# Keys' groups: the squares of the values' weights behind the seventh high part and the first snapshot, their scale behind the seventh low part

## The chip, the cores and the metric

The kernel runs on one core of a Trainium2 chip. The metric is the device time of one execution in microseconds, as the median of several runs. TensorE is PE in the profile, VectorE is DVE, ScalarE is ACT, GpSimd is POOL, SyncE is SP.

## The reference

Two decoder layers over 512 tokens of width 2048. Each layer normalises its input, sends it through one input projection, and feeds three groups of heads: a gated short convolution, stick-breaking attention with 8 heads, and gated linear attention with 4 heads. The three outputs are joined, go through an output projection and are added to the input. Cut to what matters here:

```python
h = _rmsnorm(x, norm_g)
proj = h @ w_in                       # [512, 2048] x [2048, 7696]
(cv_h, cv_b, cv_c, cv_g,
 sb_q, sb_k, sb_v, sb_g,
 gl_q, gl_k, gl_v, gl_g, gl_lr) = jnp.split(proj, split_points, axis=-1)
...
q = _rmsnorm(sb_q.reshape(b, s, SB_HEADS, SB_HD), sb_qn_g)
k = _rmsnorm(sb_k.reshape(b, s, SB_HEADS, SB_HD), sb_kn_g)
v = sb_v.reshape(b, s, SB_HEADS, SB_HD)
y_sb = _stick_breaking(q, k, v) * jax.nn.silu(sb_g)
...
mix = jnp.concatenate([y_conv, y_sb, y_gla], axis=-1)
return x + mix @ w_out
```

All is in float32, and the kernel reaches that precision with float16 matmuls.

## The kernel before, in words

**Groups.** The weights are taken in groups of 256 columns, in an order fixed in `specs` and `names`. In each layer, for each of the four pairs of attention heads j, the groups come as `v j` (values), `g j` (gate), `q j` (queries), `k j` (keys). Behind `k 3` comes `conv h 1`. So behind each of the eight keys' groups (four in each of two layers) stands a group whose weights are not of the quick kind: `v 1`, `v 2`, `v 3` or `conv h 1`. The text calls them the values' weights.

**High and low parts.** A float32 weight is scaled by a power of two and split into a float16 high part (ACT, a scaled copy) and a float16 low part (DVE, the scaled weight minus the high part). The scale comes from the sum of the squares of the group's weights: two squares on ACT with accumulators (`wmax`, L383), a reduction over the partitions on POOL (`wscale`, L399), and four small operations on DVE (L402 to L417).

**Two kinds of groups.** A plain group has two high parts and two low parts of 128x2048 (L454, L461), and `project_toks` multiplies with them, 192 matmuls (L712 to L714, or L701 to L703 where columns come first). A quick group (queries, keys, gates) uses a Strassen-like scheme with seven products on half-size blocks. `wsums` forms sums of weight blocks in place on DVE (L516 to L532) and splits seven blocks into high and low parts of 128x1024 (L507, L508). The seventh has buffers of its own, `w7h` and `w7l`; its input comes from the sum on L532. `project_quick` makes the seven products (L796 for queries and keys, 48 matmuls each; L793 where columns come first) in two PSUM banks. Between them ACT takes snapshots of partial sums (L808, L812, L815) and DVE combines (L809, L816 to L821). The first snapshot reads what product 1 left, in a bank shared with product 2, and product 5 goes on accumulating there. The second reads what product 4 left, and product 7 goes on there.

**What runs beside a keys' group.** While TensorE works on `k j`, ACT and DVE finish the splits of the keys' own weights, square and scale the queries (L1361, L1379, L1383, L1384), and prepare the next group's weights: squares, scale, parts. Weights are staged in two buffers (`st`); the load of the group after next (L362, issued by POOL) waits until the seventh low part, the last reader of the buffer, is done. Behind the group the keys are squared (L1361), scaled, split (L1383, L1384) and transposed by DMA (L1388), and the scores of the heads (L1270) need them.

**What sets the order.** Nothing of this part is placed by hand. A planner runs the program through a timeline of its own and fills each engine's queue by priority; `tc.high_priority()` lifts the squares, the scale and the parts of the next group above the rest. `order(a, b)` only says that the planner must not place `a` ahead of `b`: it makes no semaphore. `weights()` leaves two hooks for the group, called by the projection as it emits its matmuls. The first hook emits the squares of the next group's weights (`squares`), the second their scale and parts (`parts_of`), each ordered behind the matmul that it is given. In `project_quick` the first hook is called at the third matmul of product 1, the second after product 2:

```python
if start and t == kk == 0 and i == 2 and o is pa:
    hook(mm)
...
prod(pa, w11, a11, True)
hook(prod(pb, wT2, s_, False))
S.activation(y12, za, AF.Copy)
```

Of the kernel before, what the change touches and what calls it, by code (L numbers as in the profile page):

```python
# [10 lines left out]
AF = mybir.ActivationFunctionType  # L11
ALU = mybir.AluOpType
# [31 lines left out]
def hybrid_trunk(ctx, tc, x, norm_g, w_in, conv_w, conv_b, sb_qn_g, sb_kn_g,  # L44
                 gla_w_up, gla_b_up, gla_on_g, w_out, out):
    nc = tc.nc
    V, S, G, T = nc.vector, nc.scalar, nc.gpsimd, nc.tensor
# [27 lines left out]
    def sm(n, tag, bufs=None):  # L75
        return small.tile([P, n], F32, tag=tag, name=nm(tag), bufs=bufs or 1 + (tag in TWICE))
# [7 lines left out]
    def bank(pool, tag):  # L84
        return pool.tile([P, 512], F32, tag=tag, name=nm("ps" + tag))
# [109 lines left out]
    def order(a, b):  # L195
        tc.add_manual_dep(a.ins, b.ins.name, mybir.DependencyInfo(
            mybir.DependencyClass.NoSync, mybir.DependencyReason.DATA), reason="order")
# [119 lines left out]
    names = []  # L317
# [25 lines left out]
    loaded = {}  # L343
    cursor = [0]

    staged, whole, narrow, peak, scales = {}, {}, {}, {}, {}

    def junk(n):

# [42 lines left out]
    def wscale(i):  # L392

        l, src, cols = specs[i]

        m = sm(1, "wq")
        if i:
            gm = sm(2 + (i in narrow), "wgm")
            G.partition_all_reduce(gm, peak.pop(i), P, RED.add)  # L399
            if i in narrow:  # L400
                V.tensor_tensor(gm[:, 0:1], gm[:, 0:1], gm[:, 2:3], ALU.add)
            first = V.tensor_tensor(m, gm[:, 0:1], gm[:, 1:2], ALU.add)  # L402
        else:

            ps = bank(psm, "m")[:, :1]
            pk = peak.pop(i)
            first = None
            for j, (a, b) in enumerate(((ones, pk[:, 0:1]), (ones, pk[:, 1:2]), (pk[:, 2:3], pk[:, 2:3]))):
                T.matmul(ps, a.to_broadcast([P, P]), b, start=j == 0, stop=j == 2)
            V.tensor_scalar(m, ps, 2.0 ** -120, None, ALU.max)  # L410
        V.tensor_scalar(m.bitcast(I32), m.bitcast(I32), 0x7F000000, 1, ALU.bitwise_and, ALU.logical_shift_right)

        lift = int(i in quick)
        sc = sm(1, "ws")
        V.tensor_scalar(sc.bitcast(I32), m.bitcast(I32), -1.0, float((204 - lift) << 23), ALU.mult, ALU.add)  # L415
        u = sm(1, "wu", bufs=6)
        V.tensor_scalar(u.bitcast(I32), m.bitcast(I32), (outoff[l] if src is w_out else inoff)[lift][:, l:l + 1],  # L417
                        None, ALU.add)
        loaded[i] = ([], u)
        scales[i] = sc  # L420
        return first
# [37 lines left out]
    def wlo(i, h):  # L459
        wh, wl = loaded[i][0][h]  # L460
        V.scalar_tensor_tensor(wl[:, :, :GW], staged[i][h], scales[i], wh[:, :, :GW], ALU.mult, ALU.subtract)  # L461
        if i in narrow:
            V.scalar_tensor_tensor(wl[:, :, GW:], narrow[i][:, h * HK:(h + 1) * HK, :], scales[i], wh[:, :, GW:],
                                   ALU.mult, ALU.subtract)

    def squares(i, mm):

        with tc.high_priority():
            for h in range(2):
                a = wmax(i, h)  # L470
                if not h:
                    order(a, mm)
                if ksq:
                    order(a, ksq[0])
            ksq.clear()

    def parts_of(i, mm):

        with tc.high_priority():
            order(wscale(i), mm)  # L480
            if i in quick:
                wsums(i)
                return
            for h in range(2):
                whi(i, h)
                wlo(i, h)

    def hook(mm):

        if hooks:  # L490
            hooks.pop(0)(mm)

    def wsums(i):

        sc = scales[i]
        b11, b12, b21, b22 = (whole[i][:, r::2, c * P:(c + 1) * P] for r in range(2) for c in range(2))
        parts = loaded[i][0]
        for _ in range(3):
            a = [wpool.tile([P, HK, GX], F16, tag=t, name=nm(t)).rearrange("p k c -> p (k c)") for t in ("wh", "wl")]
            parts.extend([p_[:, n * HK * P:(n + 1) * HK * P] for p_ in a] for n in range(2))  # L500
        parts.append([wk([P, HK * P], t, 1, dt=F16) for t in ("w7h", "w7l")])
        for n in range(7):
            parts[n] = [a.rearrange("p (k c) -> p k c", c=P) for a in parts[n]]

        def split(b, n):
            h_, l_ = parts[n]
            hi = S.activation(h_, b, AF.Copy, scale=sc)  # L507
            V.scalar_tensor_tensor(l_, b, sc, h_, ALU.mult, ALU.subtract)  # L508
            return hi


        if specs[i][1] is w_out:
            split(b11, 0)
            V.tensor_tensor(b11, b11, b12, ALU.add)
            split(b22, 2)
            V.tensor_tensor(b12, b12, b22, ALU.add)  # L516
            V.tensor_tensor(b22, b11, b22, ALU.add)
            split(b22, 1)
            split(b12, 3)
            V.tensor_tensor(b22, b22, b21, ALU.add)  # L520
            split(b21, 4)
            split(b11, 5)
            split(b22, 6)
            return
        split(b11, 0)
        split(b22, 2)
        V.tensor_tensor(b22, b12, b22, ALU.add)  # L527
        split(b22, 1)
        V.tensor_tensor(b11, b22, b11, ALU.subtract)
        split(b11, 3)  # L530
        split(b21, 4)
        V.tensor_tensor(b21, b22, b21, ALU.add)  # L532
        split(b12, 5)
        split(b21, 6)
# [150 lines left out]
    for l in range(depth):  # L685
# [92 lines left out]
        def project_quick(src, sums, y, cols):  # L778

            (w11, wT2, w22, wT3, w21, wt1, wT4), u = weights()  # L780
            (pa, pb), (pd, pf) = ([bk[:, n * GW:(n + 1) * GW] for n in range(2)]
                                  for bk in [bank(psp, "p") for _ in range(2)])
            a11, a12, a22 = ([a[:, 2 * r:2 * r + 2, c::2, :] for a in src] for r, c in ((0, 0), (0, 1), (1, 1)))
            s_, a21_22, a12_s, a11_21 = sums

            def prod(o, w, a, start, stop=False):
                for t in range(1 if cols else 2):
                    for kk in range(HK):
                        for i, (p_, q_) in enumerate(((0, 0), (0, 1), (1, 0))):
                            st_ = start and t == kk == i == 0  # L790
                            en = stop and kk == HK - 1 and i == 2
                            if cols:
                                mm = T.matmul(o, w[q_][:, kk, :], a[p_][:, :, kk, :], start=st_, stop=en,  # L793
                                              skip_group_check=True)
                            else:
                                mm = T.matmul(o[:, t * P:(t + 1) * P], a[p_][:, t, kk, :], w[q_][:, kk, :], start=st_,  # L796
                                              stop=en, skip_group_check=True)
                            if start and t == kk == 0 and i == 2 and o is pa:
                                hook(mm)
                return mm  # L800

            y11, y12, y21, y22 = (
                y[:, c, r * GW:(r + 1) * GW] if cols else y[:, 2 * r:2 * r + 2, c * P:(c + 1) * P]
                for r in range(2) for c in range(2))
            za, zb, zd, zf = (a if cols else a.rearrange("p (t c) -> p t c", c=P) for a in (pa, pb, pd, pf))
            prod(pa, w11, a11, True)
            hook(prod(pb, wT2, s_, False))
            S.activation(y12, za, AF.Copy)  # L808
            V.tensor_tensor(y21, zb, y12, ALU.subtract)  # L809
            prod(pf, w22, a12_s, True)  # L810
            prod(pd, wT3, a11_21, False)
            S.activation(y22, zd, AF.Copy)  # L812
            prod(pa, w21, a12, False)
            prod(pb, wt1, a21_22, False, True)
            S.activation(y11, za, AF.Copy)  # L815
            V.tensor_tensor(y12, zb, y12, ALU.subtract)  # L816
            V.tensor_tensor(y22, y12, y22, ALU.subtract)
            lastmm[0] = prod(pd, wT4, a22, False, True)
            V.tensor_tensor(y12, zf, y12, ALU.add)
            yield 0, u  # L820
            V.tensor_tensor(y21, zd, y21, ALU.subtract)  # L821
            yield 2, u
# [148 lines left out]
        for p in range(2):  # L971
# [3 lines left out]
            a = wk([P, seq], "ga")  # L975
# [26 lines left out]
        for tag in ("qT", "kT"):  # L1002
            o = wk([P, 2, seq], tag)
# [14 lines left out]
            s_ = sm(1, "gas")  # L1018
# [42 lines left out]
        for p in range(2):  # L1061
# [4 lines left out]
            for li, h in enumerate(LEV[:-1]):  # L1066
                b = li % 2
# [32 lines left out]
            hi, lo = src16[1]  # L1100
# [38 lines left out]
            for a, o in zip(ax, (aps[:, :, :256], aps[:, :, 256:], aps2[:, :, :256])):  # L1139
                hi, lo = (a[:, i].rearrange("p (h c) -> p h c", h=2) for i in range(2))  # L1140
# [179 lines left out]
        for j in range(4):  # L1320
# [17 lines left out]
            s_ = mixscale(2 + j, m, "b", 12.0)  # L1338
# [3 lines left out]
            for n in range(2):  # L1342
# [11 lines left out]
                for b in range(2):  # L1354
# [4 lines left out]
                    for i in range(4):  # L1359
                        cs = slice(i * P, (i + 1) * P)  # L1360
                        a = S.activation(e[:, cs], rb.rearrange("p a c -> p (a c)")[:, cs], AF.Square,  # L1361
                                         accum_out=sq[:, 8 * n + 4 * b + i:8 * n + 4 * b + i + 1])
# [117 lines left out]
```

## Time and profile before

| | |
|---|---|
| median of 3 runs | 1647.73 us (1642.52 to 1655.6) |
| profiled execution, own time | 1646.43 us |
| its span | 1644.6 us |
| busy share of the span | PE 98%, DVE 87%, ACT 72%, POOL 16% |
| granted TensorE clock | 1.000 |

Times inside the profile count from the start of the span. In a timeline each row has the start, the duration, the engine, the line, the operation with what it writes and reads, the shapes, the count, and in brackets the idle time ahead of it with what ended it. Matmuls overlap in the pipeline, so 48 of them take less than 48 times the duration of one.

### The profile page before, as it was taken

The page shows a single profiled execution, that of the slowest core. Times are in us where ns is not written, and L with a number is a line of the kernel's source. Part 1 is how long each engine was busy: PE and PEld are TensorE (multiplying, and loading weights), DVE is VectorE, ACT ScalarE, POOL GpSimd, SP SyncE. Part 2 cuts the span into 40 slices and gives each one's busy share as a digit, 9 for nine tenths or more (in the row PEclk, how much of TensorE's full clock was granted, in tenths as well). Part 3 has the DMA queues.
Part 4 walks back from the last instruction along what each step waited for, and adds up shares of the span by engine and source line. Part 5 has one row for each costly group of instructions (what it writes and reads, how often), then busy time and mean ns, then how long its engine had stood idle before and what let it go on. Part 6 is the DMA issues. An engine that isn't in the chain of part 4 may idle for free.

```text
span 1644.6 us, 41938 instructions
## 1 busy us (share of the span) xinstructions
PE 1619.6 (98%) x18058; PEld 1356.1 (82%) x18058; DVE 1433.7 (87%) x2403; ACT 1192.3 (72%) x1763; POOL 270.7 (16%) x300
## 2 busy tenths in 40 slices
PE   8999999999999999999999999999999999999999
PEld 5757768989899967799986668689898989768998
DVE  7989989989898979898699899898988889878893
ACT  7668887977777776756766788788777878666571
POOL 0122021211112121111102111211121212110110
PEclk9999999999999999999999999999999999999999
DMA  7154435477868677544643544546776776894441
GB/s 260 54 129 140 93 118 114 108 160 142 166 149 167 149 167 197 171 155 142 203 120 105 129 116 116 140 83 140 151 157 153 158 158 155 174 196 141 155 155 53
DMA packets 195995, 235.97 MB, mean 143 GB/s; under 512 B 90259, under 2 KB 156125, under 8 KB 195297
## 3 DMA queue, kind: packets, MB, share of 16 engines
q0 software_dynamic: 79072, 178.27, 41.2%
q1 hardware_dynamic: 107728, 45.56, 14.6%
q10 hardware_dynamic: 9008, 9.45, 1.8%
q8 instruction: 141, 2.31, 0.6%
q14 instruction: 46, 0.37, 0.1%
HBM read 179.65 MB, written 14.68 MB: 118 GB/s over the span
## 4 chain that ended last, share of the span: by engine, by line
PE 33%; DVE 10%; ACT 4%; DMA 3%; issue 2%; SPq 0%; POOL 0%; DVEq 0%; ACTq 0%; POOLq 0%
PE psp L796 11%; PE psp L793 6%; PE psp L843 4%; PE psp L714 2%; PE psp L713 2%; PE psp L712 2%; DVE wl L508 2%; PE psp L702 1%; PE psp L701 1%; PE psp L703 1%; DMA m<-mixd 1%; ACT wh L507 1%; ACT junk L383 1%; DMA kT<-raw 1%; DVE wl L461 1%
## 5 line engine op out<-in xcount | busy, mean ns | idle before, releaser
L507 ACT ACTIVATE wh<-st,ws 128x1024 f16<-128x1024 f32 x264 | 293.8, 1144 | 168.3 <-DVE st L527 89.8
L508 DVE SCALAR_TENSOR_TENSOR wl<-st,ws,wh 128x1024 f16<-128x1024 f32 x264 | 332.1, 1280 | 24.0 <-ACT wh L507 23.8
L383 ACT ACTIVATE junk<-st 128x2048 uint8<-128x2048 f32 x150 | 285.5, 1903 | 19.4 <-DMA st<-in_w_out_dram 10.4
L793 PE MATMUL psp<-s,wh 128*128 128x256 f16 x1280 | 217.7, 273 | 0.0
L793 PEld LDWEIGHTS <-wh 128*128 128x128 f16 x1920 | 187.4, 98 | 23.4 <-issue 1.4
L796 PE MATMUL psp<-wh,s 128*128 128x128 f16 x2048 | 177.2, 219 | 0.8 <-issue 0.8
L714 PE MATMUL psp<-wh,m 128*128 128x256 f16 x640 | 174.5, 273 | 3.1 <-DVE m L1195 3.1
L793 PE MATMUL psp<-s,wl 128*128 128x256 f16 x640 | 174.3, 273 | 0.9 <-DVE wl L508 0.9
L712 PE MATMUL psp<-wh,m 128*128 128x256 f16 x640 | 174.5, 273 | 0.0
L713 PE MATMUL psp<-wl,m 128*128 128x256 f16 x640 | 174.5, 273 | 0.0
L796 PEld LDWEIGHTS <-s 128*128 128x128 f16 x3072 | 172.9, 98 | 1.2 <-issue 1.2
L796 PE MATMUL psp<-wl,s 128*128 128x128 f16 x1024 | 173.3, 219 | 0.0
L461 DVE SCALAR_TENSOR_TENSOR wl<-st,ws,wh 128x2048 f16<-128x2048 f32 x64 | 149.4, 2347 | 16.2 <-ACT wh L454 15.6
L362 POOL DMA_DIRECT2D st<-in_w_in_dram x114 | 110.9, 1051 | 256.0 <-DVE w7l L508 112.7
L454 ACT ACTIVATE wh<-st,ws 128x2048 f16<-128x2048 f32 x62 | 122.4, 1995 | 32.3 <-DVE ws L415 19.2
L796 PEld LDWEIGHTS <-m 128*128 128x128 f16 x2304 | 131.0, 98 | 2.5 <-issue 2.1
L399 POOL PARTITION_ALL_REDUCE wgm<-wm x75 | 55.6, 742 | 456.9 <-ACT junk L383 442.8
L386 POOL DMA_DIRECT2D st<-st x36 | 57.3, 1591 | 356.0 <-ACT junk L383 336.7
L793 PEld LDWEIGHTS <-wl 128*128 128x128 f16 x960 | 93.9, 98 | 13.2 <-DVE wl L508 1.4
L796 PE MATMUL psp<-wh,m 128*128 128x128 f16 x1024 | 91.5, 219 | 0.7 <-DVE ws L415 0.4
L796 PE MATMUL psp<-wl,m 128*128 128x128 f16 x512 | 87.5, 219 | 0.0
L843 PEld LDWEIGHTS <-m 128*128 128x128 f16 x768 | 75.0, 98 | 12.4 <-DMA m<-th 1.3
(443 smaller groups left out, 4136.8 us busy)
## 6 DMA issues: line engine op xcount, KB each, us to landing
st<-in_w_in_dram POOLq DMA_DIRECT2D x114, 1024.0 KB, 8.4
st<-in_w_out_dram POOLq DMA_DIRECT2D x32, 1024.0 KB, 9.3
st<-st POOLq DMA_DIRECT2D x36, 512.0 KB, 6.7
st<-in_w_in_dram SPq DMA_DIRECT2D x6, 1024.0 KB, 12.0
mixd<-g POOLq DMA_DIRECT2D x20, 256.0 KB, 8.0
x<-in_x_dram SPq DMA_DIRECT2D x4, 1024.0 KB, 4.9
qT<-in_x_dram ACTq DMA_DIRECT2D x8, 512.0 KB, 6.8
qT<-xs ACTq DMA_DIRECT2D x8, 512.0 KB, 4.0
```

The source lines that it names most:

```text
L362: load = queue.dma_start(s_, src[l, h * HK * P:(h + 1) * HK * P, c0:c0 + GW].rearrange("(k p) n -> p k n", p=P), max_dma_last_dim=1024)
L383: sq = S.activation(junk(HK * GW).rearrange("p (k n) -> p k n", k=part.shape[1]), part, AF.Square, accum_out=peak[i][:, h:h + 1])
L454: hi = S.activation(wh[:, :, :GW], staged[i][h], AF.Copy, scale=scales[i])
L461: V.scalar_tensor_tensor(wl[:, :, :GW], staged[i][h], scales[i], wh[:, :, :GW], ALU.mult, ALU.subtract)
L507: hi = S.activation(h_, b, AF.Copy, scale=sc)
L508: V.scalar_tensor_tensor(l_, b, sc, h_, ALU.mult, ALU.subtract)
L712: T.matmul(o, ah[:, t, k, :], wh[:, kk, :n], start=st_, stop=False, skip_group_check=True)
L713: T.matmul(o, ah[:, t, k, :], wl[:, kk, :n], start=False, stop=False, skip_group_check=True)
L714: return T.matmul(o, al[:, t, k, :], wh[:, kk, :n], start=False, stop=en, skip_group_check=True)
L793: mm = T.matmul(o, w[q_][:, kk, :], a[p_][:, :, kk, :], start=st_, stop=en, skip_group_check=True)
L796: mm = T.matmul(o[:, t * P:(t + 1) * P], a[p_][:, t, kk, :], w[q_][:, kk, :], start=st_, stop=en, skip_group_check=True)
L843: mm = T.matmul(o[:, :n], a_[:, t, k, :], w[k // HK][part][:, k % HK, :n], start=i == 0 and k == 0, stop=i == 2 and k == KT - 1)
```

## The change

In a keys' group the squares of the next weights are emitted later and tied behind two more places: behind the seventh high part of the keys' weights (ACT), and behind the first snapshot (ACT) in place of the third matmul. The scale of the next weights is tied behind the seventh low part of the keys' weights (DVE). `wsums` remembers these two instructions in `last7`. In every quick group the second hook is called after the first snapshot is emitted instead of ahead of it.

```diff
-    staged, whole, narrow, peak, scales = {}, {}, {}, {}, {}
+    staged, whole, narrow, peak, scales, last7 = {}, {}, {}, {}, {}, {}
...
+    def keys(i):
+        return names[i][:2] == "k "
+
     def squares(i, mm):
 
         with tc.high_priority():
...
                 if ksq:
                     order(a, ksq[0])
+                if keys(i - 1):
+                    order(a, last7[i - 1][0])
             ksq.clear()
 
     def parts_of(i, mm):
 
         with tc.high_priority():
-            order(wscale(i), mm)
+            a = wscale(i)
+            order(a, mm)
+            if keys(i - 1):
+                order(a, last7[i - 1][1])
...
             hi = S.activation(h_, b, AF.Copy, scale=sc)
-            V.scalar_tensor_tensor(l_, b, sc, h_, ALU.mult, ALU.subtract)
+            lo = V.scalar_tensor_tensor(l_, b, sc, h_, ALU.mult, ALU.subtract)
+            last7[i] = hi, lo
             return hi
...
-                            if start and t == kk == 0 and i == 2 and o is pa:
+                            if start and t == kk == 0 and i == 2 and o is pa and not behind:
                                 hook(mm)
...
+            behind = keys(cursor[0] - 1)
             prod(pa, w11, a11, True)
-            hook(prod(pb, wT2, s_, False))
-            S.activation(y12, za, AF.Copy)
+            mm = prod(pb, wT2, s_, False)
+            a = S.activation(y12, za, AF.Copy)
+            if behind:
+                hook(a)
+            hook(mm)
```

## The prediction

> **What bounds the kernel now.** I read the page's busy row first, then the waits of TensorE over the whole run, then the windows around single keys' groups, and last the chain of waits and the timelines inside two of these groups.
>
> ```profile
> PE 1619.6 (98%) x18058; PEld 1356.1 (82%) x18058; DVE 1433.7 (87%) x2403; ACT 1192.3 (72%) x1763; POOL 270.7 (16%) x300
> PE psp L714 <- DVE m L1195: 3.1, 2, 2.1
> PE psz L244 <- ACT qp L234: 3.1, 1, 3.1
> PE psp L793 <- DVE w7l L508: 2.1, 2, 1.1
> PE psp L796 <- DVE ws L415: 0.8, 2, 0.4
> PE psz L1270 <- DMA kT<-raw: 0.4, 1, 0.4
> ```
>
> TensorE (PE) is busy for 1619.6 of 1644.6 us, so all its idle time is 25.0 us, or 1.5% of the span. A change that only reorders work of ScalarE (ACT) and VectorE (DVE) can win no more than that. The waits (total, times, longest) show where it is: start-up (L244), the output projection (L714), a seventh low part in two convolution groups (L793). The changed code can directly touch only the last two rows: 0.8 us in two waits inside a keys' group and 0.4 us ahead of its scores.
>
> Now one window per site, each from the start of a keys' group to the end of the group behind it (columns: length, then busy time and instructions of PE, PEld, DVE, ACT, POOL).
>
> ```profile
> 313.90:355.50 41.60, 41.10 (x540) 38.24 (x538) 34.60 (x65) 31.25 (x60) 7.09 (x8) 1.00 0.66 147
> 1120.70:1162.30 41.60, 40.82 (x538) 38.01 (x536) 34.99 (x65) 32.10 (x62) 7.67 (x9) 1.00 0.74 147
> 1204.80:1246.40 41.60, 41.60 (x548) 39.12 (x546) 34.17 (x59) 31.32 (x62) 9.26 (x10) 1.00 0.77 175
> 1196.58 27.06 PE psp L796 x480
> 1223.64 1.65 PE psm L1310 x18
> 1246.24 1.63 PE psz L1270 x12
> ```
>
> There are two kinds of site. In the first keys' group of each layer (first two rows) TensorE loses 0.5 and 0.8 us; in a later one (third row) it works 41.60 of 41.60 us. The other later ones have the same order of instructions, so I reckon two first sites and six later ones. The chain's pieces (start, length) give TensorE's own clock for the later site: 480 matmuls in 27.06 us are 56.4 ns each, so one product of 48 takes 2.71 us. The keys' seven products (19.0 us) end at 1223.64 and began at 1204.7; product 2 ended at 1210.1, product 4 at 1215.5, product 7 begins at 1220.9. The next group (values) begins at 1223.64 + 1.65 = 1225.29 and the scores at 1246.24. Every delivery below is held against these times.
>
> **The change part by part.** No instruction is added or taken away, and a tie made by `order` is a place in an engine's queue, without a semaphore. What moves is: two squares with their two accumulator reads (ACT), the partition reduction (POOL), four small scale operations (DVE), and behind them two high parts (ACT) and two low parts (DVE) of the values' weights. This is the later site as it is:
>
> ```profile
> 1207.60 1.90 ACT L383 ACTIVATE junk<-st 128x2048 uint8<-128x2048 f32 x1
> 1210.08 1.90 ACT L383 ACTIVATE junk<-st 128x2048 uint8<-128x2048 f32 x1
> 1211.97 1.14 ACT L507 ACTIVATE w7h<-st,ws 128x1024 f16<-128x1024 f32 x1
> 1213.60 0.37 ACT L808 ACTIVATE kT<-psp 128x256 f32<-128x256 f32 x1
> 1215.03 2.00 ACT L454 ACTIVATE wh<-st,ws 128x2048 f16<-128x2048 f32 x1
> 1218.48 2.00 ACT L454 ACTIVATE wh<-st,ws 128x2048 f16<-128x2048 f32 x1
> 1220.37 0.37 ACT L812 ACTIVATE kT<-psp 128x256 f32<-128x256 f32 x1
> 1208.35 1.22 DVE L532 TENSOR_TENSOR st<-st 128x1024 f32<-128x1024 f32 x1
> 1213.25 1.28 DVE L508 SCALAR_TENSOR_TENSOR w7l<-st,ws,w7h 128x1024 f16<-128x1024 f32 x1
> 1217.06 2.35 DVE L461 SCALAR_TENSOR_TENSOR wl<-st,ws,wh 128x2048 f16<-128x2048 f32 x1
> 1221.13 2.35 DVE L461 SCALAR_TENSOR_TENSOR wl<-st,ws,wh 128x2048 f16<-128x2048 f32 x1
> 1212.24 0.40 POOL L399 PARTITION_ALL_REDUCE wgm<-wm  x1 [13.94 <-ACT junk L383]
> 1214.83 1.78 POOL L362 DMA_DIRECT2D st<-in_w_in_dram  x2 [2.19 <-DVE w7l L508]
> ```
>
> The input of the seventh high part (L532) is there at 1209.57, yet the part starts at 1211.97: the second square sits ahead of it.
>
> *Seventh parts.* The high part can come 1211.97 - 1209.57 = 2.4 us earlier, the low part too (about 1210.9 instead of 1213.25). TensorE needs them at 1220.9 and has them at 1214.5 today, so here this is worth 0. What follows is the POOL row: the next gate's load waits for the low part, and could be issued some 2.4 us earlier. On POOL it would pass the reduction, which is then not ready; were it queued behind, it would wait until about 1215.7, 0.9 us later than today.
>
> *Squares, scale and parts of the values' weights.* High part until 1210.7, first snapshot (ready with product 2, 1210.1) until 1211.1, two squares of about 2.0 us each until 1215.1, reduction from 1215.3. From its start to the first high part it takes 2.79 us today (1212.24 to 1215.03), with the low part of 1.28 in between, so some 1.5 without: the first high part starts at 1216.8 instead of 1215.03. Then it and the second end at 1218.8 and 1220.8, the low parts at 1221.2 and 1223.5. TensorE asks for the first pair at 1225.29 and for the second half a group later. Margin 4.1 us, cost 0.
>
> *Second snapshot.* Product 7 accumulates on what L812 reads, and that ends today at 1220.74, 0.2 us ahead of 1220.9. If it stays behind the second high part it ends at 1221.2 and TensorE waits 0.3 us. But ACT has a hole now, from 1215.1 to 1216.8, and the snapshot is ready at 1215.5. Between 0 and 0.3 us a site I take 0, because of that hole.
>
> The first sites are tighter; this is the one of layer 1:
>
> ```profile
> 1127.01 1.22 DVE L532 TENSOR_TENSOR st<-st 128x1024 f32<-128x1024 f32 x1
> 1128.53 1.13 ACT L507 ACTIVATE w7h<-st,ws 128x1024 f16<-128x1024 f32 x1
> 1130.77 1.28 DVE L508 SCALAR_TENSOR_TENSOR w7l<-st,ws,w7h 128x1024 f16<-128x1024 f32 x1
> 1131.96 0.42 DVE L809 TENSOR_TENSOR kT<-psp,kT 128x256 f32<-128x256 f32 x1
> 1132.44 0.22 PE L796 MATMUL psp<-wh,m 128*128 128x128 f16 x1 [0.38 <-DVE ws L415]
> 1132.48 3.90 ACT L454 ACTIVATE wh<-st,ws 128x2048 f16<-128x2048 f32 x2 [0.18 <-DVE ws L415]
> 1136.29 0.36 ACT L812 ACTIVATE kT<-psp 128x256 f32<-128x256 f32 x1
> 1140.37 0.43 DVE L816 TENSOR_TENSOR kT<-psp,kT 128x256 f32<-128x256 f32 x1
> 1140.48 0.27 PE L712 MATMUL psp<-wh,m 128*128 128x256 f16 x1
> 1132.35 1.78 POOL L362 DMA_DIRECT2D st<-in_w_in_dram  x2 [3.46 <-DVE w7l L508]
> 1133.25 8.83 DMA st<-in_w_in_dram
> 1153.01 9.31 DMA kT<-raw
> 1162.36 1.52 PE L1270 MATMUL psz<-kT,qT 128*128 128x512 f16 x10 [0.44 <-DMA kT<-raw]
> ```
>
> Here L532 ends at 1128.23, so the high part gains only 0.3 us. The wait of 0.38 us ahead of product 5 is named after a scale operation, but the operation that has just ended is L809 (1132.38), queued behind the seventh low part. The high part would end at 1129.4 and let the low part begin 1.4 us earlier if the planner uses it. Both first sites have that wait: 0 to 0.76 us gained; I take **0.4**. The chain's load and transpose pieces show a second gain: gate load (8.83 us), squares, the keys' own squares behind them, transpose (9.31 us), scores with a wait of 0.44 us. An earlier low part advances that load. But the keys' last result is due only near 1142 (four combinations of 0.4 us from 1140.37 on), where the load lands too (1133.25 + 8.83), so of 0 to 0.44 us I take **0.2**.
>
> Against it: behind the high part (1129.4), the snapshot (0.3) and two squares (4.0) it is 1133.7, the first high part starts near 1135.4 (1.7 later, as above) instead of 1132.48, both are done by 1139.3, the low parts by 1139.7 and 1142.0. TensorE starts the values at 1140.48 and takes the first low part with its second matmul: margin 0.8 us, cost 0 to 1 us if other ACT work slips in. The second low part reaches past 1140.37, where the keys' combinations (L816) start; moved behind it they would be up to 1.7 us late, and the 0.44 us wait shows this path has no margin. The second snapshot, placed behind the high parts, would end at 1139.7; product 7 begins at 1140.48 - 2.71 = 1137.8, so 1.9 us. Per first site these costs overlap on TensorE: 0 to about 2. I take 0, since ACT again has a hole (1133.7 to 1135.4) in which the snapshot fits.
>
> **Sum.** -0.4 - 0.2 = -0.6 us against the profiled execution's own 1646.43 us (span 1644.6 and 1.8 around it). That execution is 1.30 us under the median of the three runs, so on the median 1647.73 - 0.6 = **1647.1 us**. The three runs spread from 1642.52 to 1655.6, so about 1%, or 16 us, is what a measurement can tell from no change.
>
> **Rivals.**
>
> *Slower: the second snapshot stays behind the values' high parts.* It was there at both kinds of site (1218.48 and then 1220.37; 1132.48 and then 1136.29), which speaks for it; the new hole on ACT speaks against. It decides once the second high part ends after product 7 is due (1220.9; 1137.8). Price: six sites at 0.3 and two at 1.9 us, 5.6 us, giving 1653.3. A late value weight then hides in the same waits.
>
> *Faster: the early low part pays through the loads.* If all of it comes true, both 0.38 us, the 0.44 us and the 2.1 us of the seventh low parts of later convolution groups go: 3.3 us, 1644.4. Against it: those two convolution waits are in other groups, and their low part is queued on DVE, not short of data.
>
> *The ties change nothing on TensorE.* The squares move, every margin swallows it, and the two small waits stay: 1647.7. For it stands the third window, with no idle time to remove.
>
> *TensorE has hidden room.* If its matmuls were spaced by something that the other engines' order relieves, the sum would be far off: the rest between span and weight-load time in the three windows is 3.4, 3.6 and 2.5 us, so up to some 22 us over eight sites, 1626. Against it:
>
> ```profile
> 1544.98 75.04 PE psp L796 x1344
> ```
>
> There 1344 matmuls of the same kind run 55.8 ns apart, as against 56.4 ns here; at most 0.6 ns x 336 = 0.2 us a group is to be had. The Trainium skill, "Perfetto Trace Analysis", section "Identifying the Most-Contended Engine", says that matmul occupancy is a poor measure of headroom and that weight-load occupancy should be used; by it the 82% of the first row would leave room, and this rival would be the likely one. The spacing in this trace says otherwise.
>
> **How the numbers follow.** Forecast 0.62 (1647.1), slower by the snapshot 0.17 (1653.3), faster by the loads 0.10 (1644.4), no effect 0.10 (1647.7), hidden room 0.01. The range must also bear the scatter of a median of runs that spread by 13 us, some 3 to 4 us each way around each case: 1641 to 1656. No single case but the last reaches 1%; with the scatter I give faster 0.01, same 0.96, slower 0.03.
>
> **What would show it.** Right: in the later sites the seventh high part starts within 0.2 us of L532's end, the first snapshot comes next, then the two squares; gate loads issued some 2 us earlier; the window of a later site still 41.60 us of TensorE. The second snapshot before the first high part of the values' weights shows the hole was used; behind the second, with a TensorE wait ahead of product 7, the slower rival. A wait of L712 or L713 for `wh` or `wl` shows the values' weights late, a longer one at L1270 the keys late. Wrong altogether: waits in groups that the ties do not name, which would mean that the planner laid the whole program out anew, for better or worse.

## The result and the profile after

The kernel after takes 1654.17 us (median of 21 runs, 1649.29 to 1661.39), the kernel before, in runs beside it, 1643.95 us (21 runs, 1638.96 to 1655.95). The ratio is 1.0058, with a 95% interval of 1.0043 to 1.0073: slower by some 9.5 us. The profiled executions have spans of 1654.1 and 1644.6 us. The lines of the changed code have moved: L712 and L713 are now L721 and L722, L796 is L805, L816 is L829, L1270 is L1283, L1310 is L1323, L1361 is L1374.

The busy row of the page, and the longest waits of TensorE over the whole run (total, times, longest):

```profile
PE 1621.7 (98%) x18058; PEld 1356.3 (82%) x18058; DVE 1433.4 (87%) x2403; ACT 1191.8 (72%) x1763; POOL 271.4 (16%) x300
PE psp L722 <- DVE wl L461: 4.2, 2, 2.1
PE psz L1283 <- DMA kT<-raw: 3.9, 8, 0.6
PE psp L723 <- DVE m L1208: 2.4, 2, 2.0
PE psp L721 <- ACT wh L454: 0.8, 2, 0.4
```

Work and instructions are the same; TensorE's idle time is 1654.1 - 1621.7 = 32.4 us, where it was 25.0. Two places make it: the values' first parts, late by 0.4 (high) and 2.1 us (low) at each of the two first sites, 5.0 us in all, and the scores, whose waits for the keys' transposes grew from 0.4 us once to 3.9 us in eight. Together 8.5 us are new. Against them stand 0.7 us less in the output projection (L723, once 3.1) and some 0.4 us in small rows. The other 2.1 us of the span are a larger busy sum (1621.7 against 1619.6). Behind the low part's wait of layer 0's first site (2.1 us, until 336.24) TensorE ran slowly for a while; behind the same wait of layer 1 (until 1147.47) it did not (window, length, busy time and matmuls of TensorE; then its granted clock, the DMA engines' busy share, GB/s):

```profile
336.00:340.00 4.00, 3.76 (x21) 0.61 0.40 84
1148.00:1152.00 4.00, 4.00 (x39) 1.00 0.17 36
```

At a granted clock of 0.61 it did 21 matmuls, where 39 fill 4 us at 1.00; the next 4 us had 37. I estimate that this cost some 1.8 us (3.76 us less 21 x 4.00/39, and two matmuls more). The busy sums of the profiled runs below lie between 1616 and 1623 for the same 18058 matmuls, so not every difference between them is the clock.

One window per kind of site, from the start of the keys' group to just ahead of the scores (columns as in the prediction: PE, PEld, DVE, ACT, POOL; then granted clock, DMA share, GB/s): the first row is layer 1's first keys' group, stretched to 44.30 us; the second is the later site that the prediction showed.

```profile
1124.20:1168.50 44.30, 41.51 (x549) 38.65 (x547) 35.66 (x67) 30.13 (x60) 6.79 (x8) 1.00 0.59 132
1212.30:1253.90 41.60, 41.60 (x549) 39.08 (x547) 34.04 (x59) 31.28 (x62) 7.70 (x9) 1.00 0.81 176
```

At the first site 2.8 us are missing on TensorE. At the later one it works through 41.60 of 41.60 us at the same clock; what it loses there comes behind the window, at the scores.

**The first site (layer 1).** The timeline of the kernel after: ACT first, then POOL, DVE and TensorE.

```profile
1132.50 1.15 ACT L515 ACTIVATE w7h<-st,ws 128x1024 f16<-128x1024 f32 x1 [0.50 <-DVE bpc L189]
1133.82 1.90 ACT L383 ACTIVATE junk<-st 128x2048 uint8<-128x2048 f32 x1
1135.72 0.30 ACT L1374 ACTIVATE e<-raw 128x128 f32<-128x128 f32 x1
1137.47 0.71 ACT L925 ACTIVATE g<-za,gsmix 128x512 f16<-128x512 f32 x1
1138.08 1.90 ACT L383 ACTIVATE junk<-st 128x2048 uint8<-128x2048 f32 x1
1139.97 0.37 ACT L825 ACTIVATE kT<-psp 128x256 f32<-128x256 f32 x1
1143.03 3.89 ACT L454 ACTIVATE wh<-st,ws 128x2048 f16<-128x2048 f32 x2 [1.74 <-DVE ws L415]
1140.04 0.85 POOL L928 DMA_DIRECT2D mixd<-g  x1 [1.87 <-DVE g L926]
1140.86 0.41 POOL L399 PARTITION_ALL_REDUCE wgm<-wm  x1
1141.32 1.23 DVE L1397 SCALAR_TENSOR_TENSOR qp<-raw,qp 128x1024 f16<-128x1024 f32 x1 [1.58 <-ACT qp L1396]
1142.47 0.15 DVE L402 TENSOR_TENSOR wq<-wgm 128x1 f32<-128x1 f32 x1
1145.06 4.62 DVE L461 SCALAR_TENSOR_TENSOR wl<-st,ws,wh 128x2048 f16<-128x2048 f32 x2 [1.70 <-ACT wh L454]
1145.08 0.27 PE L721 MATMUL psp<-wh,m 128*128 128x256 f16 x1 [0.39 <-ACT wh L454]
1147.47 0.27 PE L722 MATMUL psp<-wl,m 128*128 128x256 f16 x1 [2.12 <-DVE wl L461]
1169.11 0.38 PE L1283 MATMUL psz<-kT,qT 128*128 128x512 f16 x1 [0.63 <-DMA kT<-raw]
```

Several delays follow one another. The first square (from 1133.82) ends at 1135.72, but the second begins at 1138.08: the planner put six squares of the queries (L1374, until 1137.47) and the high part of a branch's output (L925) into these 2.36 us. The squares end at 1139.98, yet the reduction starts at 1140.86, behind the issue of a DMA in POOL's queue (L928). It ends at 1141.27, yet the scale begins at 1142.47, behind the low part of the queries (L1397), which had itself waited 1.58 us for ACT's L1396. The first high part then starts at 1143.03, after 1.74 us without work on ACT, and TensorE, which is done with the keys at 1144.69 (1145.08 - 0.39), waits for both first parts of the values.

**The later site.** ACT's, DVE's and POOL's rows there, TensorE's first work behind the keys, and the keys' transposes on SP's queue:

```profile
1217.27 1.15 ACT L515 ACTIVATE w7h<-st,ws 128x1024 f16<-128x1024 f32 x1 [1.37 <-DVE st L541]
1218.74 0.31 ACT L1374 ACTIVATE e<-raw 128x128 f32<-128x128 f32 x1 [0.32 <-DVE raw L830]
1219.34 0.36 ACT L818 ACTIVATE kT<-psp 128x256 f32<-128x256 f32 x1
1219.61 1.90 ACT L383 ACTIVATE junk<-st 128x2048 uint8<-128x2048 f32 x1
1221.50 0.30 ACT L1374 ACTIVATE e<-raw 128x128 f32<-128x128 f32 x1
1222.67 1.90 ACT L383 ACTIVATE junk<-st 128x2048 uint8<-128x2048 f32 x1
1226.12 0.37 ACT L825 ACTIVATE kT<-psp 128x256 f32<-128x256 f32 x1
1226.39 3.89 ACT L454 ACTIVATE wh<-st,ws 128x2048 f16<-128x2048 f32 x2
1228.42 4.62 DVE L461 SCALAR_TENSOR_TENSOR wl<-st,ws,wh 128x2048 f16<-128x2048 f32 x2 [0.82 <-ACT wh L454]
1232.95 0.42 DVE L829 TENSOR_TENSOR kT<-psp,kT 128x256 f32<-128x256 f32 x1
1241.61 1.22 DVE L1392 TENSOR_TENSOR kT<-kT,qr 128x1024 f32<-128x1024 f32 x1
1220.20 1.77 POOL L362 DMA_DIRECT2D st<-in_w_in_dram  x2 [14.27 <-DVE w7l L516]
1230.99 0.82 PE L1323 MATMUL psm<-th,v 128*128 128x256 f16 x6
1243.95 6.77 SPq L1401 DMA_TRANSPOSE kT<-raw  x2
```

The keys' combination, their scaling, their transposes and TensorE's first work behind them in the kernel before:

```profile
1223.39 0.42 DVE L816 TENSOR_TENSOR kT<-psp,kT 128x256 f32<-128x256 f32 x1
1232.06 1.22 DVE L1379 TENSOR_TENSOR kT<-kT,qr 128x1024 f32<-128x1024 f32 x1
1234.39 6.79 SPq L1388 DMA_TRANSPOSE kT<-raw  x2
1223.47 0.60 PE L1310 MATMUL psm<-th,v 128*128 128x256 f16 x4
```

The order on ACT is the one that the ties ask for: seventh high part, first snapshot (L818), the two squares, second snapshot (L825), high parts. Squares of the queries (L1374) stand ahead of the snapshot and fill most of the 1.16 us between the two squares. To see what it costs, the two kernels are laid one upon the other at the end of the keys' products, taken as the start of TensorE's next work: 1223.47 before (L1310) and 1230.99 after (L1323). The prediction's 1223.64 for this point is the end of the last matmul, 0.17 us later. The combinations began 0.08 us ahead of it and now begin 1.96 us behind it, because both low parts (4.62 us on DVE), which stand ahead of them in both kernels, now come later. The keys' scaling began 8.59 and now 10.62 us behind that point, the transposes' issue 10.92 and now 12.96. So the 2.0 us are handed on whole to the transposes. At the scores of this site, due 22.6 us behind the same point, only a last 0.2 us comes out; the other sites of the layer lose more. In windows around the four sites of layer 1 the waits at L1283 for the transposes sum to 1.1 us (first site), 0.2 (this one), 1.0 and 1.1. With 0.5 us at one later site of layer 0 these are the 3.9 us: 1.1 at a first site (0.4 before) and 2.8 at later ones.

### The profile page after: what moved, and what is told of

The parts are those of the page before. It is cut to its first block, busy times and chain, and to the rows that moved or that the text cites. A ratio compares the mean times of both kernels' runs of the same rounds, so it can differ in the third digit from the quotient of the medians.

```text
span 1654.1 us, 41938 instructions
## 1 busy us (share of the span) xinstructions
PE 1621.7 (98%) x18058; PEld 1356.3 (82%) x18058; DVE 1433.4 (87%) x2403; ACT 1191.8 (72%) x1763; POOL 271.4 (16%) x300
## 4 chain that ended last, share of the span: by engine, by line
PE 19%; DVE 15%; DMA 7%; ACT 6%; issue 4%; POOL 1%; SPq 0%; DVEq 0%; POOLq 0%; ACTq 0%
PE psp L805 5%; PE psp L856 4%; DMA st<-in_w_in_dram 4%; DVE wl L516 4%; PE psp L802 3%; ACT junk L383 1%; PE psp L723 1%; PE psp L722 1%; PE psp L721 1%; DMA m<-mixd 1%; DVE w7l L516 1%; PE psp L712 1%; PE psp L710 1%; PE psp L711 1%; DVE za L1299 1%
## 5 line engine op out<-in xcount | busy, mean ns | idle before, releaser
L805 PE MATMUL psp<-wh,s 128*128 128x128 f16 x2048 | 177.1, 219 | 0.0
L723 PE MATMUL psp<-wh,m 128*128 128x256 f16 x640 | 174.5, 273 | 2.4 <-DVE m L1208 2.4
L722 PE MATMUL psp<-wl,m 128*128 128x256 f16 x640 | 174.5, 273 | 2.1 <-DVE wl L461 2.1
L721 PE MATMUL psp<-wh,m 128*128 128x256 f16 x640 | 174.5, 273 | 0.4 <-ACT wh L454 0.4
L805 PE MATMUL psp<-wl,s 128*128 128x128 f16 x1024 | 173.3, 219 | 0.0
L805 PEld LDWEIGHTS <-s 128*128 128x128 f16 x3072 | 172.9, 98 | 0.3
L805 PEld LDWEIGHTS <-m 128*128 128x128 f16 x2304 | 130.9, 98 | 2.2 <-issue 1.9
L805 PE MATMUL psp<-wh,m 128*128 128x128 f16 x1024 | 91.5, 219 | 0.5 <-DVE raw L822 0.3
L805 PE MATMUL psp<-wl,m 128*128 128x128 f16 x512 | 87.5, 219 | 0.0
```

The source lines that it names most:

```text
L721: T.matmul(o, ah[:, t, k, :], wh[:, kk, :n], start=st_, stop=False, skip_group_check=True)
L722: T.matmul(o, ah[:, t, k, :], wl[:, kk, :n], start=False, stop=False, skip_group_check=True)
L723: return T.matmul(o, al[:, t, k, :], wh[:, kk, :n], start=False, stop=en, skip_group_check=True)
```

## The experiments

Theory A is what these lines say: the values' parts come late, the first low part stops TensorE at the first sites, and the second low part pushes the keys' combinations and so the scores. Theory B, the rival: the next gate load, which is issued earlier now, gets in the way of the keys' transposes. Edits are against the kernel after, if nothing else is said. TensorE's queue is the same in all of these kernels but the two with the second square alone, where at each first site one matmul of the values stands ahead of the keys' last product. As runs shown together had their own runs of the kernel before (medians 1641.76 to 1642.22), ratios are compared, not times.

**The first sites alone.**

```diff
     def keys(i):
-        return names[i][:2] == "k "
+        return names[i] == "k 0"
```

> The complement: the ties in the two first keys' groups (k 0 of each layer) only. Theory A: two waits of some 2.1 us at L722 and two of 0.4 us at L721 stay, so about 5 to 5.5 us slower than before; the scores of the later sites wait for nothing. Theory B: hardly slower, 0 to 1 us, since the load moves by only some 0.4 us there.

Measured: 1649.51 us (6 runs) against 1641.8, ratio 1.0041 (1.0025 to 1.0058). Its waits of TensorE:

```profile
PE psp L722 <- DVE wl L461: 4.2, 2, 2.1
```

Two of the eight sites carry 0.41 of the 0.58%, with the wait of the kernel after unchanged (0.41% of 1641.8 is 6.7 us; the waits that are new there sum to 5.0 and, at their scores, 0.4). In this profile the granted clock fell behind both waits, to 0.71 in the window 336 to 340 us and to 0.75 in 1148 to 1152, some 1.8 us each by the estimate above, so clock and waits together can make up the loss. B, which had 0 to 1 us here, is out at these sites.

**The later sites alone.**

```diff
-        return names[i][:2] == "k "
+        return names[i][:2] == "k " and names[i] != "k 0"
```

> The ties of the change in the six later keys' groups only; the two first ones (k 0) stay as before. Theory A (the values' weights come late: their first low part stops TensorE in the first sites, 2.5 us each; their second low part pushes the keys' combinations and with them the scores in the later sites): about 4 to 5 us slower than before instead of 10; no wait at L722 behind a keys' group, but the waits of the scores (L1283) of 0.2 to 1.1 us a site stay. Theory B (the gate loads, issued some 2 us earlier, collide with the queries' and keys' transposes): these loads move mainly in the later sites, so nearly the whole 10 us stay.

Measured: 1643.91 us (12 runs) against 1641.8, ratio 1.0017 (0.9996 to 1.0037).

```profile
PE psz L1283 <- DMA kT<-raw: 3.2, 7, 0.6
```

The wait for `wl` is gone and the scores' wait is there; 0.4 of the 3.2 us are the old wait of layer 1's first site, so 2.8 are new. By the ratio alone this part can't be told from no change; its middle, 0.17% or 2.8 us, fits the wait. That the middles of the two parts add up to the whole, 0.41 + 0.17 = 0.58%, is closer than intervals of some 0.2% each way can show.

**The second low part behind the keys' combinations.** This leaves the squares, the scale, the high parts and the gate loads as they are and takes only the second low part out of the combinations' way.

```diff
-                wlo(i, h)
+                if not (h and keys(i - 1)):
+                    wlo(i, h)
...
-            V.tensor_tensor(y21, zd, y21, ALU.subtract)
+            b = V.tensor_tensor(y21, zd, y21, ALU.subtract)
+            if behind:
+                with tc.high_priority():
+                    order(wlo(cursor[0], 1), b)
```

> The change as it is, but the second low part of the values' weights is emitted behind the keys' last combination and tied there, so that it no longer stands ahead of the keys' combinations on VectorE. Theory A: the combinations start about 2 us earlier against TensorE, the waits of the scores (3.9 us) go, the waits in the first sites stay: 6 to 7 us slower than before. Theory B: the loads are where they were, 10 us slower as with the change.

Measured: 1646.85 us (12 runs) against 1641.8, ratio 1.0029 (1.0018 to 1.0041). A wait, and DVE at the later site:

```profile
PE psp L724 <- DVE wl L461: 4.2, 2, 2.1
1224.76 2.35 DVE L461 SCALAR_TENSOR_TENSOR wl<-st,ws,wh 128x2048 f16<-128x2048 f32 x1 [0.82 <-ACT wh L454]
1227.03 0.42 DVE L831 TENSOR_TENSOR kT<-psp,kT 128x256 f32<-128x256 f32 x1
1228.68 2.34 DVE L461 SCALAR_TENSOR_TENSOR wl<-st,ws,wh 128x2048 f16<-128x2048 f32 x1
```

The combinations stand between the two low parts, and of the scores' waits one of 0.27 us is left. The gate loads are as early as in the kernel after (at the later site 10.78 us ahead of the end of the keys' products, there 10.79), which speaks against B. What remains is the first low part: 5.0 us in the waits, 0.29% of 1642 = 4.8 us in the ratio, somewhat less than the 6 to 7 us that A had.

**Later sites alone, with the late second low part**, both edits together.

> The ties in the six later keys' groups only, with the second low part of the values' weights behind the keys' last combination there. Theory A: both costs are gone, so within 1 us of before, or up to 1 us faster. Theory B: about 3 us slower, as with the ties in the later groups alone.

Measured: 1640.13 us (11 runs) against 1641.76, ratio 0.9993 (0.9984 to 1.0002). The waits at the sites are those of the kernel before:

```profile
PE psp L807 <- DVE ws L415: 0.8, 2, 0.4
PE psz L1288 <- DMA kT<-raw: 0.4, 1, 0.4
```

With both places closed nothing is left of the loss, though the squares are tied at six of the eight sites and six gate loads come as early as with the change (10.79 us ahead at the later site). This run decides against B.

**Only the squares' tie behind the seventh high part**, without the scale's tie. The first hook is back at the third matmul; the second is still called behind the first snapshot, as in all of these kernels.

```diff
             order(a, mm)
-            if keys(i - 1):
-                order(a, last7[i - 1][1])
...
-            behind = keys(cursor[0] - 1)
+            behind = False
```

> Only the tie of the squares behind the seventh high part; the first hook is at the third matmul again and the scale isn't tied. Theory A: the squares end earlier than with the change by one snapshot and the queries' squares around it, about 1 to 2 us, so the waits at the first sites shrink but don't vanish and the scores hardly wait: 2 to 5 us slower than before. Theory B: the seventh low part and with it the loads are as early as with the change, so 10 us slower.

Measured: 1652.05 us (6 runs) against 1641.8, ratio 1.0059 (1.0041 to 1.0078), much more than I had expected from A.

```profile
PE psz L1281 <- DMA kT<-raw: 7.4, 11, 1.6
PE psp L720 <- DVE wl L461: 1.6, 2, 0.8
1224.03 3.88 ACT L454 ACTIVATE wh<-st,ws 128x2048 f16<-128x2048 f32 x2
1230.58 0.42 DVE L827 TENSOR_TENSOR kT<-psp,kT 128x256 f32<-128x256 f32 x1
1228.22 0.60 PE L1321 MATMUL psm<-th,v 128*128 128x256 f16 x4
```

The size is B's, the places are A's: the combinations begin 2.36 us behind the end of the keys' products, and the first low part is late at the first sites. The gate loads can't be the cause: they are issued 10.79 us ahead of that end, as in the two runs just above with the late second low part, in which the scores hardly waited. This one tie, without the other two, is thus enough for the whole loss, in another mixture: the combinations come 0.4 us later still, and the scores wait 7.4 us instead of 3.9.

**Only the second square tied behind the seventh high part.** The edit is the one before, with `if h and keys(i - 1):` at the squares' tie, so that the first square may go ahead.

> Only the second square is tied behind the seventh high part; first square, hooks and scale as before. This brings the seventh low part and the gate load nearly as early as with the change, but the squares end only some 0.6 us later than before. Theory A (late parts): the values' high and low parts keep their places, no new wait at L720 or at the scores, within 1 us of before. Theory B (early gate loads collide): the waits of the scores appear as with the change, 3 to 4 us slower.

Measured: 1641.07 us (11 runs) against 1641.76, ratio 0.9995 (0.9977 to 1.0013). Gate load and the end of the keys' products (L1321) at the later site:

```profile
1212.09 1.79 POOL L362 DMA_DIRECT2D st<-in_w_in_dram  x2
1221.79 0.82 PE L1321 MATMUL psm<-th,v 128*128 128x256 f16 x6
PE psz L1281 <- DMA kT<-raw: 0.6, 2, 0.5
```

The load is issued 9.70 us ahead of the keys' end. Before it was 1223.47 - 1214.83 = 8.64 us, after 1230.99 - 1220.20 = 10.79. So this kernel has half of the earlier load, seventh parts that come early, and no loss: what the seventh parts needed was the way past one square.

**Only the scale's tie.** No tie at the squares, the first hook at the third matmul.

```diff
-                if keys(i - 1):
-                    order(a, last7[i - 1][0])
...
-            behind = keys(cursor[0] - 1)
+            behind = False
```

> Only the scale is tied behind the seventh low part; squares and hooks as before. The scale moves by about the length of that low part, 1.3 us, and what stands behind it. Theory A: low parts come some 1 to 2 us later than before and not the 4 to 6 of the change: waits of the scores of up to 1 us a site, little in the first sites, 1 to 4 us slower. Theory B: the seventh low part comes only some 0.5 us earlier, so hardly slower, 0 to 1 us.

Measured: 1644.25 us (12 runs) against 1641.76, ratio 1.0025 (1.0012 to 1.0038). Its waits at the scores are 0.4 us in all, as before, and at the sites it has none for `wl`, so its 4 us are not explained by A, though they lie in A's range. At the later site its combinations begin 1.26 us behind the end of the keys' products, and the scores don't wait for it. Its profiled execution has the output projection's reload wait (2.7 us), as that of before has (3.1), and those of some other kernels have not. Here, unlike in the kernel before, the granted clock fell behind it (0.92 in the window 1476 to 1480 us, 0.66 in 1480 to 1484). One profile can't tell whether that belongs to the tie. This stays open.

**Only the snapshot's tie.** Both `last7` ties out, the hooks as in the kernel after.

```diff
-                if keys(i - 1):
-                    order(a, last7[i - 1][0])
...
-            if keys(i - 1):
-                order(a, last7[i - 1][1])
```

> Only the tie of the squares behind the first snapshot; no tie to the seventh parts. The planner's queues come out as with the whole change. Theory A (late parts), which puts all on where the squares stand: the same waits at L721, L722 and at the scores as with the change, 9 to 10 us slower than before. Theory B (early gate loads): the same too; this run only says which of the three ties acts.

Measured: 1652.51 us (9 runs) against 1642.22, ratio 1.0068 (1.0046 to 1.0090).

```profile
PE psp L718 <- DVE wl L461: 4.2, 2, 2.1
PE psz L1279 <- DMA kT<-raw: 3.7, 7, 0.7
```

The queues of all five engines are row for row those of the kernel after. With the squares behind the first snapshot, the two other ties decide nothing: that one place makes the change. As the kernel with the seventh high part's tie alone shows, it is not the only place that costs as much.

**The kernel before, with the late second low part**, as a control of that edit.

> The kernel before, with no tie, but with the second low part of the values' weights behind the keys' last combination. Theory A: the keys' combinations start up to 2 us earlier than before and the 0.4 us wait of the scores in layer 1 goes: 0 to 0.5 us faster, not to be told from before. Theory B: nothing changes for the loads, the same as before.

Measured: 1641.7 us (12 runs) against 1641.76, ratio 0.9998 (0.9980 to 1.0015). Where the second low part was in time, moving it brings nothing. Against A's expectation the 0.4 us wait of layer 1's scores stays, though the combinations there begin 1.6 us earlier; so it did not hang on them. This kernel also calls the second hook behind the first snapshot in every quick group, as the change does, and that alone costs nothing that these runs can tell.

**The second square alone, with the late second low part**, the most promising mixture of the edits.

> The second square behind the seventh high part, and the second low part of the values' weights behind the keys' last combination; the rest as before. Theory A: seventh low part and gate load early, scores early, no part late: the waits of the scores are gone, 0 to 1 us faster than before, hardly to be told from it. Theory B: 3 to 4 us slower.

Measured: 1641.62 us (12 runs) against 1642.22, ratio 1.0004 (0.9985 to 1.0023). The scores still wait 0.5 us once. No version found is faster than the kernel before by more than its measurement is uncertain.

**What the runs settle.** The late parts of the values' weights and the combinations behind them carry the loss: sites with neither have none, but for the open case of the scale's tie, and each goes when it is taken away by itself. Early gate loads are no cause at the sizes tried. The traces point to a third part of the loss, TensorE's clock behind the wait at the first sites. All four profiled kernels with that wait of 2.1 us (the kernel after, the first sites alone, the late second low part, the snapshot's tie) have the slow stretch at layer 0's first site; none of the eight without it has one there. Over all executions the granted clock agrees: its mean is 0.9970 to 0.9978 in each of these four, and 0.9987 to 0.9994 in the others, with 0.9990 to 0.9992 for the kernel before. The stretch in the profile of the kernel after, the only one in it, goes with 0.999, so I estimate between one and two more of them per execution than before, 2 to 3 us of the loss. No run tested the clock by itself. Why the planner filled the space between the squares with other work was seen, not tested.

## Why the prediction was wrong

- **The bound** held: TensorE is busy 98% of the span before and after, and waits at the sites, with the clock behind them, moved the time. The rival of hidden room did not show: at the later site TensorE did 548 matmuls in 41.60 us before and 549 after, with the other engines' work in another order. By the Trainium skill, "Perfetto Trace Analysis", section "Identifying the Most-Contended Engine", headroom on TensorE is judged, among others, by the busy share of weight loading, and 82% would leave some. The trace of the kernel after has the same 82%, and in the keys' products a matmul every 0.06 us, as before, and does not bear that out.
- **The seventh parts** were right: the high part starts at 1217.27, as its input is ready, and the gate load comes 10.79 - 8.64 = 2.15 us earlier against the keys' end (some 2.4 forecast), worth nothing.
- **The squares, scale and parts step failed**, and it is the one that decides. I added up bare durations, with a first high part at the later site at 1216.8, 1223.47 - 1216.8 = 6.7 us ahead of the keys' end. It came 1230.99 - 1226.39 = 4.60 us ahead, 2.1 us late: the first square began 1.0 us later than in my sum, the second another 1.1 us, both with squares of the queries ahead of them on ACT; from the reduction to the high part the 1.5 us held (1224.83 to 1226.39). At the first site I had 1140.48 - 1135.4 = 5.1 us ahead of the values' first matmul. Without its wait that matmul would have started at 1144.53, behind the keys' last one at 1144.47, and the part came 1144.53 - 1143.03 = 1.5 us ahead, 3.6 us late. I had named the gaps that I meant ACT to fill with a snapshot, and not counted what else would fill them: there, the squares of the queries and a branch's output between the squares, the issue of a DMA ahead of the reduction on POOL, a low part of the queries ahead of the scale on DVE.
- **"Margin 0.8 us, cost 0 to 1 us if other ACT work slips in"** thus became 2.5 us at each first site, and more where the clock fell behind it. I named the mishap, capped it at 1 us without a row, and then took 0.
- **"Margin 4.1 us, cost 0"** at the later sites tested the wrong reader. TensorE did get the parts in time there, as forecast. But the second low part has the keys' combinations behind it on DVE. I had it end at 1223.5, level with 1223.39 where they began, and had priced that chain ("up to 1.7 us late") for the first sites only, and there at nothing. The combinations came 2.0 us later, which cost 2.8 us at the later sites' scores.
- **The second snapshot** was right, at both kinds of site: 1226.12 and 1139.97, ahead of the first high part. So the slower rival, with its 1653.3 us the nearest of the priced cases, didn't occur; that the result lies near it is chance. The range, too, holds 1654.17 us only because it was widened for the scatter of single runs: by the sum the change was 0.6 us faster, and it is some 9.5 us slower. Nor is 1% the least that can be told from no change, as the prediction had it; with 21 runs of each kernel 0.58% was.
- **The gains** of 0.4 and 0.2 us were mis-sized: the first came to some 0.3 us, the second turned round, to 1.1 us of waits at the scores of layer 1's first site where there had been 0.44.

## What to carry to other kernels

A step that is moved passes every queue that its chain goes through, and at each of them something may have taken its place: price it by the next item of ACT, POOL and DVE, not by the sum of its own durations. A gap that the sum opens on an engine is an offer to the planner, which fills it with whatever is next, and what it fills in can stand ahead of the step that was meant to go there. A short wait of TensorE can cost more than its length, where its clock falls behind it. A part that reaches its reader in time can still be late for whoever stands behind it on the same engine, so each delivery is held against both.

## What the runs showed of the hardware

Behind a wait of 2.1 us (with one of 0.4 us just ahead of it) TensorE's granted clock could fall for some microseconds: 21 matmuls in 4 us at 0.61, as against 39 at 1.00. It did so in each of the four profiles with that wait at layer 0's first site, and at layer 1's, behind a wait of the same length, in one of the four only (0.75 in the window 1148 to 1152 us, the first sites alone).
